# Second layer's values for four heads in one pass: 512 moving columns, three sets of rows in turn

## The chip, the cores and the metric

The kernel runs as one program on one core of a Trainium2 chip. The metric is the device time of one execution in microseconds (us), the median of several runs. A profile of one further execution gives the instructions of each engine: TensorE (PE, with its weight loads listed as PEld), VectorE (DVE), ScalarE (ACT), GpSimd (POOL) and the queue of SyncE (SPq), which issues most of the transfers.

## The reference, cut to what matters

Two decoder layers on 512 tokens of width 2048. The first is gated linear attention and is not touched. The second is multi-head latent attention with 16 heads; the part that matters is how queries, keys and values of the heads come out of two latent rows of width 512, and the attention over them:

```
q = (rms_norm(c_q, g_qa) @ w_qb).reshape(B, S, MLA_HEADS, MLA_NOPE + MLA_ROPE)
kv = (rms_norm(c_kv, g_kva) @ w_kvb).reshape(B, S, MLA_HEADS, MLA_NOPE + MLA_V)
k_nope, v = kv[..., :MLA_NOPE], kv[..., MLA_NOPE:]
...
s = jnp.einsum('bqhd,bkhd->bhqk', qb, k).astype(jnp.float32) * scale
p = jax.nn.softmax(s, axis=-1).astype(v.dtype)
return jnp.einsum('bhqk,bkhv->bqhv', p, v)
```

In w_kvb each head has 256 columns: first 128 for its key, then 128 for its value. The output of the 16 heads is multiplied by a gate and goes through an output projection.

## The kernel before

All large products are made in float32 accuracy by splitting each operand into a high part (type fp32r) and a low rest, and adding three products: high by high, low by high, high by low. The helper mm3 (L123 to L127) issues these three matmuls, so each product of a 128 by 128 stationary tile with its moving rows costs three matmuls and three weight loads, on lines 125, 126 and 127. A matrix from DRAM is loaded in chunks of 1024 numbers a row by the SP queue (tag "raw", three buffers), cast to its high part by ACT (L110, or L827 in the second layer's pairs) and turned into its low part by DVE (L111, L828); the split chunks have four buffers for each part. A finished accumulator of 128 by 512 is split in the same way by split_from: ACT on L174, DVE on L175.

The method mla runs the second layer. After the latent rows cq and ckv and the gates, the heads go in eight pairs. project(p) makes queries, keys and values of pair p, attend(p) does the attention of its two heads; the order in the program is project(0), attend(0), project(1), attend(1) and so on, and after attend(7) the output projection (accumulators yo_acc). The order in which each engine gets its instructions isn't this one: a planner with a simulated timeline (TileContext with schedule_with_timeline_sim) lays it down when the kernel is built, and it moves later work forward into gaps where data and buffers allow. Each engine then runs its own list in that fixed order.

One project(p) holds:

- three accumulators q_acc of 512 columns, 12 matmuls each (four latent tiles by three). The first of them to be made carries the rotary part; its evacuation (L861 to L870) goes through two buffers of the tag "tmp", of which there are six, shared with the softmax rows "pr" of the attention.
- two accumulators k_acc, one for each head, 12 matmuls each with the latent rows (512 columns) as the moving side.
- the values, two accumulators v_acc. Here the latent rows are the stationary side (128 tokens at a time) and the weights move: for each of four blocks of 128 tokens and each of four latent tiles, three matmuls with 256 moving columns, 128 for each of the pair's two heads. Two token blocks share one accumulator. These are 48 matmuls in a pair and 384 in the layer.

The weights for keys and values of a pair come as two chunks by pair_chunk (L816 to L829), each with four transfers of 128 KB. Each chunk holds the keys' and the values' columns of both heads for two latent tiles.

The accumulators named come from a pool of three (tag "mm"). Results lie in rows of act_hi and act_lo, 16 rows of 128 by 512 each, which held the layer's input before. With b = 0 for even pairs and 6 for odd ones, rows b and b+1 hold the queries, b+2 and b+3 the keys, b+4 and b+5 the values (so 4 and 5, or 10 and 11); 12 and 13 hold the rotary queries of even and odd pairs, 14 the rotary key, and 15 is free after the gates. A pair's rows are written again two pairs later, when their last readers are through: for queries and keys the scores (sc, five matmuls for each of four blocks of tokens in a head), for values the product of probabilities and values (o_t).

attend(p) does for each head: scores, mask, maximum, exponential and scaling (L908 to L918, on DVE and ACT), transposition of the probabilities by PE (pt, L927, single matmuls of 128 columns), their split, and the 12 matmuls o_t.

At the end of mla each head's gated output is split into y_hi and y_lo (L729, L730). Head 0's pair of tiles takes the buffers b24 and b25, heads 1 to 8 those of the latent rows, head 9 those of cosine and sine, heads 10 to 15 rows 0 to 5 of act_hi and act_lo. The output projection begins with head 0.

Of the kernel before, what the change touches and what calls it, by code (L numbers as in the profile page):

```python
# [14 lines left out]
F32 = DT.float32  # L15
FR = DT.float32r
# [7 lines left out]
P = 128  # L24
S = 512
D = 2048
ST = S // P
# [12 lines left out]
NOPE = 128  # L40
ROPE = 64
RANK = 512
RK = RANK // P
# [27 lines left out]
class Trunk:  # L71
# [744 lines left out]
    def pair_chunk(self, w, c0, hd, cut, k0):  # L816
# [11 lines left out]
        nc.vector.tensor_tensor(lo, raw, hi.bitcast(F32), ALU.subtract)  # L828
        return hi, lo  # L829

    def project(self, p):

        nc, v, a = self.nc, self.nc.vector, self.a
        par = p % 2
        if p == 0:
            self.key_rope_split()
            self.pairs = {}
        ah, al = self.act_hi, self.act_lo
        b = par * 6
        qn = [(ah[:, b + i, :], al[:, b + i, :]) for i in range(2)]  # L840
        kn = [(ah[:, b + 2 + i, :], al[:, b + 2 + i, :]) for i in range(2)]
        vv = [(ah[:, b + 4 + s // 2, (s % 2) * 256:(s % 2) * 256 + 256],
               al[:, b + 4 + s // 2, (s % 2) * 256:(s % 2) * 256 + 256]) for s in range(ST)]
        qr = [ah[:, 12 + par, :], al[:, 12 + par, :]]
        self.pairs[p] = (qn, kn, vv, qr)

        ps = [self.acc(f"q_acc{i}") for i in range(3)]
        ch = [self.pair_chunk(a["l1_mla_w_qb"], p * 2 * (NOPE + ROPE), NOPE + ROPE, NOPE, k0)
              for k0 in (0, 2)]
        for i in (2, 0, 1):  # L850
            c = slice(i * P, (i + 1) * P)
            for k in range(RK):
                wh, wl = ch[k // 2]
                self.mm3(ps[i], wh[:, k % 2, c], wl[:, k % 2, c], self.cq[0][k], self.cq[1][k],
                         k == 0, k == RK - 1)
            if i < 2:
                self.split_from(ps[i], *qn[i])
            else:
                sw = self.tmp([P, S], F32, "qr_sw")
                for g in range(4):  # L860
                    nc.scalar.copy(sw[32 * g:32 * g + 32], ps[i][32 * (g ^ 1):32 * (g ^ 1) + 32, :])  # L861
                t = self.tmp([P, S], F32, "qr_t")
                v.tensor_tensor(t, ps[i], self.cos, ALU.mult)
                v.tensor_tensor(sw, sw, self.sin, ALU.mult)
                v.tensor_tensor(t, t, sw, ALU.add)
                A, B = slice(0, ROPE), slice(ROPE, P)
                nc.scalar.copy(qr[0][A], t[A])
                v.tensor_tensor(qr[0][B], t[A], qr[0][A].bitcast(F32), ALU.subtract)
                nc.scalar.copy(qr[1][B], t[B])
                v.tensor_tensor(qr[1][A], t[B], qr[1][B].bitcast(F32), ALU.subtract)  # L870

        ch = [self.pair_chunk(a["l1_mla_w_kvb"], p * 4 * NOPE, 2 * NOPE, NOPE, k0) for k0 in (0, 2)]
        for i in range(2):
            pk = self.acc(f"k_acc{i}")
            c = slice(i * P, (i + 1) * P)
            for k in range(RK):
                wh, wl = ch[k // 2]
                self.mm3(pk, wh[:, k % 2, c], wl[:, k % 2, c], self.ckv[0][k], self.ckv[1][k],
                         k == 0, k == RK - 1)
            self.split_from(pk, *kn[i])  # L880
        for s2 in range(2):
            pv = self.acc(f"v_acc{s2}")
            for i in range(2):
                r = slice((s2 * 2 + i) * P, (s2 * 2 + i + 1) * P)
                for k in range(RK):
                    wh, wl = ch[k // 2]
                    self.mm3(pv[:, i * 256:(i + 1) * 256], self.ckv[0][k][:, r], self.ckv[1][k][:, r],
                             wh[:, k % 2, 256:512], wl[:, k % 2, 256:512], k == 0, k == RK - 1)
            self.split_from(pv, ah[:, b + 4 + s2, :], al[:, b + 4 + s2, :])

    def attend(self, p):
        nc, v, te = self.nc, self.nc.vector, self.nc.tensor
# [90 lines left out]
```

## Time and profile before

| what | value |
|---|---|
| median of three runs | 1489.88 us (1489.2 to 1490.59) |
| the profiled execution | 1490.05 us |
| its span, from the first to the last instruction | 1488.3 us |
| granted TensorE clock | 0.999 |
| instructions | 18065 |
| matmuls v_acc<-pw in the second layer | 384 with 256 columns, from 1065.4 to 1288.5 us |

So the profiled execution lies within the runs, 0.17 us above their median, and 1.75 us of it lie outside the span. In the rows of the profile the first number of a listing is the start of an instruction in microseconds from the span's start and the second its duration; since matmuls overlap in the array, what one costs is read from the distance to the start of the next, not from its duration.

### The profile page before, as it was taken

How to read it: one execution, taken by the hardware profiler on the slowest of the kernel's cores; microseconds unless marked ns; L12 is line 12 of the kernel's file. 1: busy time of each engine (PE TensorE's matmuls, PEld its weight loads, DVE VectorE, ACT ScalarE, POOL GpSimd, SP SyncE). 2: the span in 40 equal slices, each digit the busy share in tenths (PEclk: the TensorE clock that was granted, in tenths of full speed). 3: DMA queues.
4: the chain of work that ended last, by engine and by line, in shares of the span. 5: the costliest groups of instructions: out<-in, count | busy, mean ns of one | idle time of the engine just before them, and what ended most of it. 6: DMA issues, size and time to landing. Idle time of an engine off the chain costs nothing.

```text
span 1488.3 us, 18065 instructions
## 1 busy us (share of the span) xinstructions
PE 1472.6 (99%) x7050; PEld 1235.8 (83%) x7050; DVE 738.0 (50%) x1229; ACT 625.7 (42%) x1109; POOL 32.5 (2%) x67
## 2 busy tenths in 40 slices
PE   8999999999999999999999999999999999999998
PEld 6788888888888888888888888888888998888886
DVE  7553644354435454443365444333577777763334
ACT  7432631243124323232254344324666676752221
POOL 2000000000000000100011000000000000000000
PEclk9999999999999999999999999999999999999999
DMA  7323233323331333433262333333322112135223
GB/s 258 104 85 101 70 95 90 100 71 88 97 100 57 100 99 113 134 118 124 92 212 76 107 98 89 99 99 93 83 72 56 51 50 80 59 127 180 92 96 114
DMA packets 110918, 149.85 MB, mean 101 GB/s; under 512 B 17632, under 2 KB 58784, under 8 KB 109808
## 3 DMA queue, kind: packets, MB, share of 16 engines
q1 hardware_dynamic: 107280, 136.86, 30.2%
q0 software_dynamic: 3264, 11.73, 2.3%
q8 instruction: 55, 0.90, 0.3%
q14 instruction: 31, 0.25, 0.1%
q10 hardware_dynamic: 288, 0.09, 0.0%
HBM read 140.08 MB, written 8.59 MB: 100 GB/s over the span
## 4 chain that ended last, share of the span: by engine, by line
PE 95%; DMA 2%; DVE 1%; ACT 1%; issue 1%; SPq 0%; DVEq 0%; ACTq 0%
PE acc L127 11%; PE acc L126 11%; PE acc L125 11%; PE yo_acc L125 8%; PE yo_acc L127 8%; PE yo_acc L126 8%; PE v_acc L127 5%; PE v_acc L126 5%; PE v_acc L125 5%; PE o_t L126 1%; PE o_t L127 1%; PE q_acc L126 1%; PE q_acc L127 1%; PE q_acc L125 1%; PE o_t L125 1%; PE pt L927 1%
## 5 line engine op out<-in xcount | busy, mean ns | idle before, releaser
L111 DVE TENSOR_TENSOR w_lo<-w_raw,w_hi 128x1024 fp32r<-128x1024 f32 x159 | 194.4, 1223 | 379.9 <-ACT w_hi L110 379.5
L110 ACT CAST w_hi<-w_raw 128x1024 fp32r<-128x1024 f32 x159 | 167.3, 1053 | 429.1 <-PE acc L127 186.7
L126 PE MATMUL acc<-act_hi,w_lo 128*128 128x512 f32 x768 | 300.2, 391 | 0.0
L125 PE MATMUL acc<-act_hi,w_hi 128*128 128x512 f32 x768 | 299.6, 390 | 0.0
L127 PE MATMUL acc<-act_lo,w_hi 128*128 128x512 f32 x768 | 298.6, 390 | 0.0
L126 PEld LDWEIGHTS acc<-act_hi,w_lo 128*128 128x128 f32 x768 | 144.2, 188 | 30.6 <-issue 0.7
L127 PEld LDWEIGHTS acc<-act_lo,w_hi 128*128 128x128 f32 x768 | 144.2, 188 | 30.4 <-issue 0.7
L125 PEld LDWEIGHTS acc<-act_hi,w_hi 128*128 128x128 f32 x768 | 144.2, 188 | 29.9
L125 PE MATMUL yo_acc<-w_hi,act_hi 128*128 128x512 f32 x352 | 137.5, 391 | 0.0
L126 PE MATMUL yo_acc<-w_hi,act_lo 128*128 128x512 f32 x352 | 137.1, 389 | 0.0
L127 PE MATMUL yo_acc<-w_lo,act_hi 128*128 128x512 f32 x352 | 137.1, 391 | 0.0
L119 DVE SCALAR_TENSOR_TENSOR w_lo<-w_raw,gcol,w_hi 128x512 fp32r<-128x512 f32 x89 | 63.2, 747 | 101.1 <-ACT w_hi L118 101.0
L118 ACT ACTIVATE w_hi<-w_raw,gcol 128x512 fp32r<-128x512 f32 x89 | 59.8, 716 | 112.0 <-PE acc L127 83.8
L125 PE MATMUL v_acc<-w_hi,act_hi 128*128 128x512 f32 x256 | 100.1, 395 | 6.5 <-DVE w_hi L267 6.4
L126 PE MATMUL v_acc<-w_hi,act_lo 128*128 128x512 f32 x256 | 99.5, 393 | 0.0
L127 PE MATMUL v_acc<-w_lo,act_hi 128*128 128x512 f32 x256 | 97.0, 393 | 0.2 <-DVE w_lo L111 0.2
L127 PEld LDWEIGHTS yo_acc<-w_lo,act_hi 128*128 128x128 f32 x352 | 66.1, 188 | 13.9 <-issue 0.2
L126 PEld LDWEIGHTS yo_acc<-w_hi,act_lo 128*128 128x128 f32 x352 | 66.1, 188 | 13.7
L125 PEld LDWEIGHTS yo_acc<-w_hi,act_hi 128*128 128x128 f32 x352 | 66.1, 188 | 13.7 <-issue 0.2
L125 PEld LDWEIGHTS v_acc<-w_hi,act_hi 128*128 128x128 f32 x256 | 48.6, 190 | 17.2 <-issue 6.3
L126 PE MATMUL yo_acc<-w_hi,y_lo 128*128 128x512 f32 x160 | 62.5, 391 | 0.0
L125 PE MATMUL yo_acc<-w_hi,y_hi 128*128 128x512 f32 x160 | 62.4, 391 | 0.0
(301 smaller groups left out, 2458.4 us busy)
## 6 DMA issues: line engine op xcount, KB each, us to landing
w_raw<-in_l_gla_w_in_dram SPq DMA_DIRECT2D x63, 512.0 KB, 3.8
w_raw<-in_l_mla_w_in_dram SPq DMA_DIRECT2D x47, 512.0 KB, 3.6
w_raw<-in_l_gla_w_in_dram SPq DMA_DIRECT2D x66, 256.0 KB, 3.1
w_raw<-in_l_gla_w_out_dram SPq DMA_DIRECT2D x32, 512.0 KB, 3.8
w_raw<-in_l_mla_w_out_dram SPq DMA_DIRECT2D x32, 512.0 KB, 3.6
pw_raw<-in_l_mla_w_kvb_dram SPq DMA_DIRECT2D x64, 128.0 KB, 2.4
xo<-in_x_dram POOLq DMA_DIRECT2D x16, 256.0 KB, 6.0
x1d<-yo SPq DMA_DIRECT2D x4, 1024.0 KB, 5.6
```

The source lines that it names most:

```text
L110: nc.scalar.copy(hi, raw)
L111: nc.vector.tensor_tensor(lo, raw, hi.bitcast(F32), ALU.subtract)
L118: nc.scalar.activation(hi[:, kk, :], raw[:, kk, :], AF.Copy, scale=g)
L119: nc.vector.scalar_tensor_tensor(lo[:, kk, :], raw[:, kk, :], g, hi[:, kk, :].bitcast(F32), ALU.mult, ALU.subtract)
L125: t.matmul(out, lh, rh, start=start, stop=False)
L126: t.matmul(out, ll, rh, start=False, stop=False)
L127: t.matmul(out, lh, rl, start=False, stop=stop)
L927: te.transpose(pt[:, o:o + P], probs[i][:, j * P:(j + 1) * P], self.ident)
```

## The change

Values are now made once for two pairs, in the even project. There all four heads' value columns lie side by side, so one matmul moves 512 columns, and each block of 128 tokens fills an accumulator of its own: four accumulators of 12 matmuls. The odd project makes queries and keys alone. A finished accumulator is split in two halves, one for each pair. The new kv_chunk loads keys or values alone: the keys of a pair as one chunk with two transfers, the values of four heads as two chunks with four transfers each; it calls chunk_split (L100), which does the same cast and subtraction as pair_chunk did.

Values of up to three pairs exist at a time now, and lie in three sets of rows that are taken in turn by the pair's number: set 0 is rows 4 and 5, set 1 rows 10 and 11, set 2 is row 15 of act_hi and of act_lo for the two high parts and buffers b24 and b25 for their low parts. So pairs 2 and 5 use b24 and b25, which later take head 0's split output.

```
+    def kv_chunk(self, c0, n, k0, nk):
+        w = self.a["l1_mla_w_kvb"]
+        raw = self.wp.tile([P, nk, n * NOPE], F32, tag="raw", name="kv_raw", bufs=3)
+        for h in range(n):
+            c = c0 + h * 2 * NOPE
+            self.nc.sync.dma_start(raw[:, :, h * NOPE:(h + 1) * NOPE],
+                                   w[k0 * P:(k0 + nk) * P, c:c + NOPE].rearrange("(k p) n -> p k n", p=P))
+        return self.chunk_split(raw)
+    def value_rows(self, i):
+        ah, al = self.act_hi, self.act_lo
+        if i < 2:
+            return [(ah[:, r, :], al[:, r, :]) for r in ((4, 5), (10, 11))[i]]
+        return [(t[:, 15, :], self.slot(b, [P, S], FR, "v_lo")) for t, b in ((ah, "b24"), (al, "b25"))]
...
-        vv = [(ah[:, b + 4 + s // 2, (s % 2) * 256:(s % 2) * 256 + 256],
-               al[:, b + 4 + s // 2, (s % 2) * 256:(s % 2) * 256 + 256]) for s in range(ST)]
+        if par == 0:
+            self.v_rows = [self.value_rows((p + q) % 3) for q in range(2)]
+        vv = [tuple(t[:, (s % 2) * 256:(s % 2) * 256 + 256] for t in self.v_rows[par][s // 2])
+              for s in range(ST)]
...
-        ch = [self.pair_chunk(a["l1_mla_w_kvb"], p * 4 * NOPE, 2 * NOPE, NOPE, k0) for k0 in (0, 2)]
+        wh, wl = self.kv_chunk(p * 4 * NOPE, 2, 0, RK)
         for i in range(2):
...
-        for s2 in range(2):
-            pv = self.acc(f"v_acc{s2}")
-            for i in range(2):
-                r = slice((s2 * 2 + i) * P, (s2 * 2 + i + 1) * P)
-                for k in range(RK):
-                    wh, wl = ch[k // 2]
-                    self.mm3(pv[:, i * 256:(i + 1) * 256], self.ckv[0][k][:, r], self.ckv[1][k][:, r],
-                             wh[:, k % 2, 256:512], wl[:, k % 2, 256:512], k == 0, k == RK - 1)
-            self.split_from(pv, ah[:, b + 4 + s2, :], al[:, b + 4 + s2, :])
+        if par:
+            return
+        ch = [self.kv_chunk(p * 4 * NOPE + NOPE, 4, k0, 2) for k0 in (0, 2)]
+        for s in range(ST):
+            pv = self.acc(f"v_acc{s}")
+            r = slice(s * P, (s + 1) * P)
+            for k in range(RK):
+                wh, wl = ch[k // 2]
+                self.mm3(pv, self.ckv[0][k][:, r], self.ckv[1][k][:, r], wh[:, k % 2, :], wl[:, k % 2, :],
+                         k == 0, k == RK - 1)
+            o = (s % 2) * 256
+            for q in range(2):
+                vh, vl = self.v_rows[q][s // 2]
+                self.split_from(pv[:, q * 256:(q + 1) * 256], vh[:, o:o + 256], vl[:, o:o + 256])
```

More of the change, by code (lines that the diff above doesn't have):

```diff
@@ L876, in project @@
             for k in range(RK):
-                wh, wl = ch[k // 2]
-                self.mm3(pk, wh[:, k % 2, c], wl[:, k % 2, c], self.ckv[0][k], self.ckv[1][k],
+                self.mm3(pk, wh[:, k, c], wl[:, k, c], self.ckv[0][k], self.ckv[1][k],
                          k == 0, k == RK - 1)
             self.split_from(pk, *kn[i])
-        for s2 in range(2):
-            pv = self.acc(f"v_acc{s2}")
-            for i in range(2):
-                r = slice((s2 * 2 + i) * P, (s2 * 2 + i + 1) * P)
-                for k in range(RK):
-                    wh, wl = ch[k // 2]
-                    self.mm3(pv[:, i * 256:(i + 1) * 256], self.ckv[0][k][:, r], self.ckv[1][k][:, r],
-                             wh[:, k % 2, 256:512], wl[:, k % 2, 256:512], k == 0, k == RK - 1)
-            self.split_from(pv, ah[:, b + 4 + s2, :], al[:, b + 4 + s2, :])
+        if par:
[12 more added lines that the diff above has]
+                self.split_from(pv[:, q * 256:(q + 1) * 256], vh[:, o:o + 256], vl[:, o:o + 256])
     def attend(self, p):
```

## The prediction

> **What bounds the kernel now.** I read the page's busy times first, then PE's waits in the second layer's heads (1050 to 1350 us), then the busy times of that stage by windows.
>
> ```profile
> span 1488.3 us, 18065 instructions
> ...
> PE 1472.6 (99%) x7050; PEld 1235.8 (83%) x7050; DVE 738.0 (50%) x1229; ACT 625.7 (42%) x1109; POOL 32.5 (2%) x67
> ...
> PEclk9999999999999999999999999999999999999999
> ```
>
> ```profile
> PE k_acc L125 <- DVE qr_t L863: 0.3, 1, 0.3
> ```
>
> ```profile
> 1140.00:1160.00 20.00, 20.00 (x124) 17.99 (x123) 14.78 (x44) 13.73 (x35) 0.00 (x0) 1.00 0.18 47
> ...
> sum 300.00, PE 299.71 PEld 264.70 DVE 209.50 ACT 195.79 POOL 1.11; mean PE 19.98 PEld 17.65 DVE 13.97 ACT 13.05 POOL 0.07
> ```
>
> The reader is to see three things. PE is busy for 99% of the span at the full clock. In the 300 us around the heads its waits come to one of 0.3 us. DVE is busy for 209.5 of the 300 us (70%) and ACT for 195.8 (65%), so neither is the bound. In the heads, time is the sum of what each matmul holds the array for, and a change counts as far as it alters that sum or makes PE wait.
>
> The busy share can't tell how long a matmul holds the array, since matmuls overlap. That is read from the distance between starts in PE's listing: a run of value matmuls, one of query matmuls as the stage begins, one in the thick of it.
>
> ```profile
> 1065.37 0.28 PE L125 MATMUL v_acc<-pw_hi,ckv_hi 128*128 128x256 f32 x1
> ...
> 1068.12 0.28 PE L127 MATMUL v_acc<-pw_lo,ckv_hi 128*128 128x256 f32 x1
> ...
> 1055.04 0.39 PE L127 MATMUL q_acc<-cq_lo,pw_hi 128*128 128x512 f32 x1
> ...
> 1058.89 0.39 PE L126 MATMUL q_acc<-cq_hi,pw_lo 128*128 128x512 f32 x1
> ...
> 1105.62 0.39 PE L125 MATMUL q_acc<-cq_hi,pw_hi 128*128 128x512 f32 x1
> ...
> 1108.16 0.39 PE L127 MATMUL q_acc<-cq_lo,pw_hi 128*128 128x512 f32 x1
> ```
>
> The first two rows are the ends of 24 matmuls in a row, 23 distances: 2.75 / 23 = 0.1196 us for 256 columns. The next two have 17 distances, 3.85 / 17 = 0.2265 us for 512 columns; the last two 11 distances, 2.54 / 11 = 0.2309 us. So 512 columns cost less than twice 256, by 0.0127 or by 0.0083 us. If a matmul costs a part for its columns and a fixed part, the fixed part is 8 to 13 ns.
>
> **The value matmuls.**
>
> ```profile
> L125 PE MATMUL v_acc<-pw_hi,ckv_hi 128*128 128x256 f32 x128 | 36.4, 284 | 0.0
> ```
>
> Three lines of 128 make 384 matmuls of 256 columns: 384 x 0.1196 = 45.9 us of PE's time. Afterwards there are 4 even projects x 4 accumulators x 12 = 192 matmuls of 512 columns: 43.5 us at 0.2265, 44.3 us at 0.2309. As PE has no slack, the difference falls on the path: a saving of 2.4 or 1.6 us. I take the middle, 2.0 us, since both kinds of stretch occur in the stage. The number of columns moved is the same, 98,304; what goes is 192 fixed parts.
>
> The Trainium skill speaks against the size of this gain: its page "TensorE: Matmul & The Clock Gate", section "Back-to-back issue gap", gives the warm distance as the columns divided by 2.4 GHz plus about 2.5 ns. By that the gain would be 192 x 2.5 ns, an estimate of 0.5 us from the page. The rows above show 8 to 13 ns instead, and I go by them.
>
> **What the matmuls stand next to.** PE's lists will be laid out anew by the planner, and where a group of transpositions breaks into other work there is a price:
>
> ```profile
> 1082.42 0.30 PE L927 MATMUL pt<-cf,pr 128*128 128x128 f32 x1
> ...
> 1302.58 0.62 PE L927 MATMUL pt<-cf,pr 128*128 128x128 f32 x4
> 1302.96 0.48 PE L126 MATMUL yo_acc<-w_hi,y_lo 128*128 128x512 f32 x1
> 1303.28 0.39 PE L127 MATMUL yo_acc<-w_lo,y_hi 128*128 128x512 f32 x1
> ...
> 1340.12 0.49 PE L927 MATMUL pt<-cf,pr 128*128 128x128 f32 x3
> ```
>
> The matmul after a group holds the array for 0.32 us where 0.23 is usual: 0.09 us for each break. Between the first and the last of these rows I count 62 breaks in the listing. There can't be fewer than 48 (three groups in each of 16 heads) and I allow as many more, 76: 1.3 us either way. I take none.
>
> **Evacuation.** ACT and DVE split 32 halves of 256 columns instead of 16 accumulators of 512.
>
> ```profile
> L174 ACT CAST act_hi<-v_acc 128x512 fp32r<-128x512 f32 x16 | 9.3, 583 | 2.4 <-PE v_acc L127 2.3
> L174 ACT CAST pt_h<-pt 128x384 fp32r<-128x384 f32 x32 | 15.3, 480 | 5.3 <-PE pt L927 4.8
> L175 DVE TENSOR_TENSOR act_lo<-v_acc,act_hi 128x512 fp32r<-128x512 f32 x16 | 11.0, 686 | 5.2 <-ACT act_hi L174 5.2
> L175 DVE TENSOR_TENSOR pt_l<-pt,pt_h 128x384 fp32r<-128x384 f32 x32 | 17.2, 548 | 2.7 <-ACT pt_h L174 2.7
> ```
>
> No row has 256 columns in this form. Drawn on from 512 to 384, it comes to 377 ns on ACT and 410 ns on DVE, which is an estimate. Then ACT has 12.1 instead of 9.3 us and DVE 13.1 instead of 11.0. That is 2 to 3 us over 260, on engines with 30% to spare: nothing on the path. An accumulator is free after about 1.2 us (two casts and the last subtraction, 0.38 + 0.38 + 0.41) where it was 1.27; PE needs 12 x 0.23 = 2.7 us to fill one, and the layer fills 14 of them in two pairs as before (7 + 7, now 9 + 5). No loss.
>
> **Weights.**
>
> ```profile
> L827 ACT CAST pw_hi<-pw_raw 128x1024 fp32r<-128x1024 f32 x16 | 16.0, 1045 | 6.9 <-DMA pw_raw<-in_l_mla_w_qb_dram 4.6 <-PE v_acc L126 2.3
> L828 DVE TENSOR_TENSOR pw_lo<-pw_raw,pw_hi 128x1024 fp32r<-128x1024 f32 x16 | 19.0, 1217 | 5.0 <-ACT pw_hi L827 5.0
> ...
> w_raw<-in_l_gla_w_in_dram SPq DMA_DIRECT2D x66, 256.0 KB, 3.1
> ...
> pw_raw<-in_l_mla_w_kvb_dram SPq DMA_DIRECT2D x64, 128.0 KB, 2.4
> ```
>
> Four chunks of 1024 numbers a row for two pairs before, four after (one of keys for each pair, two of values): the same casts and subtractions. SP issues 48 transfers instead of 64, 16 of 256 KB and 32 of 128 KB; by these rows the larger land in 3.1 instead of 2.4 us. PE waits for no weights here, so this costs nothing. An even project needs five chunks where four buffers exist (two of queries, one of keys, two of values), so the last value chunk waits until a query chunk is used up: its 1.05 + 1.22 us of splitting lies behind 24 matmuls of keys, 5.5 us. Without that cover it would cost 2.3 us in each of four projects.
>
> **Rows.** Pair p's values take the set of pair p-3, where they took the rows of pair p-2. An even project therefore waits for o_t of pair p-2 at the latest (the set that pair p+1 gets), which is the wait it had. Behind the waiting splits on ACT and DVE stand the softmax steps of the attention then running. Head 0's output can't be split early any more (it was, at 1106 us): b24 and b25 are pair 5's values until its o_t is over.
>
> ```profile
> 1274.88 0.27 PE L127 MATMUL o_t<-pt_l,act_hi 128*128 128x128 f32 x1
> ...
> 1289.17 0.39 PE L125 MATMUL yo_acc<-w_hi,y_hi 128*128 128x512 f32 x1
> ```
>
> That is the last of pair 5 and the first that needs head 0: 14.3 us between them for a cast and a subtraction. Nothing on the path, unless pair 5 slips by more than that.
>
> **The sum.** 1490.05 - 2.0 = 1488.05 us for the profiled execution. That stood 0.17 above the median of the runs, so against the median: 1489.88 - 2.0 = 1487.9 us. With the bounds of both terms the forecast's own range is 1489.88 - 2.4 - 1.3 = 1486.2 to 1489.88 - 1.6 + 1.3 = 1489.6. A measurement of this kernel can tell about 0.2%, 3.0 us, from no change, and 2.0 lies below it.
>
> **Rivals.** *PE starves in odd projects (slower).* The work that fills PE's gaps while attention waits for softmax becomes uneven.
>
> ```profile
> 1130.89 0.28 PE L127 MATMUL v_acc<-pw_lo,ckv_hi 128*128 128x256 f32 x1
> ...
> 1162.73 0.28 PE L127 MATMUL v_acc<-pw_lo,ckv_hi 128*128 128x256 f32 x1
> ...
> L174 ACT CAST pt_h<-pt 128x512 fp32r<-128x512 f32 x16 | 9.4, 586 | 27.7 <-PE pt L927 27.7
> ```
>
> These are the last value matmuls of pairs 2 and 3: a pair takes 31.8 us. Without values (48 x 0.1196 = 5.7 us) an odd one has 26.1 us of PE work; an even one has 26.1 + 48 x 0.229 = 37.1. If the attention can't run faster than it does now, PE idles up to 5.7 us in each of four odd periods. Halfway, 2.9 us each, gives 11.4 - 2.0 = 9.4 us more: 1499.3. It decides from 1.25 us of idling in each odd period, where the change is 3.0 us slower. For it: queries of the next pair but one can't be evacuated before the scores of the running pair have read their rows. Against it: ACT waited 27.7 us for transpositions by PE, so the attention is paced by PE and not the other way, and DVE, busy for 209.5 / 300 of 31.8 = 22.2 us a pair, would in an odd period have 22.2 - 1.4 - 1.2 = 19.6 us of 26.1 (less two splits of values and one chunk of weights). Chance 0.18.
>
> *The planner's new order has fewer breaks.* At 48 breaks and the quiet pitch: 2.4 + 1.3 = 3.7 us saved, 1486.2. For it: longer runs of one kind; against it: nothing in the program joins transpositions. Chance 0.14.
>
> *The fixed part is small.* If value matmuls of 512 columns ran at 0.2367 us (as 0.1196 x 2 less 2.5 ns), 0.5 us would be saved: 1489.4. For it: 512 columns already differ between 0.2265 and 0.2309 by what runs beside them. Against it: no run here is that slow. It is the outcome of the page's rule above. Chance 0.06.
>
> **How the numbers follow.** The forecast has 0.62, of which 0.08 lie beyond 3.0 us. With the planner's luck, faster is 0.08 + 0.14 = 0.22. Starving gives slower, 0.16 of its 0.18; the other 0.02 and the small fixed part are within 0.2%: 0.54 + 0.02 + 0.06 = 0.62. The range, 1485.5 to 1491.5, holds the forecast, the two rivals beside it and the lightest starving (up to 0.9 us of idling in each odd period: 1487.9 + 3.6 = 1491.5), and leaves out most of that rival and a little luck beyond the bounds.
>
> **What would show it.** Right: 192 matmuls v_acc of 512 columns, 0.2265 to 0.2309 us apart; PE's waits in the heads under 1 us; all heads over some 2 us earlier; 62 breaks give or take 14. Wrong: PE waiting for q_acc, sc or o_t in odd projects, a first yo_acc that waits for y_hi, or a pitch over 0.235.

## The result: slower, by half a per cent

The changed kernel takes 1497.06 us (median of six runs, 1496.63 to 1499.72) against 1489.81 for the kernel before: 1.0052 times as long, with a 95% interval of 1.0042 to 1.0062. That is 7.25 us more, outside the predicted range and on the other side from the forecast. The profiled execution, with 1499.72 us, is the longest of the six, 2.7 us above their median. Medians here and below leave out two executions far longer than the others of their kernel (3558 us in e8, 1633 us in e14).

The page of the changed kernel, and PE's waits in the heads (1050 to 1350 us):

```profile
span 1497.9 us, 17673 instructions
...
PE 1475.7 (99%) x6858; PEld 1227.4 (82%) x6858; DVE 737.6 (49%) x1245; ACT 627.9 (42%) x1125; POOL 32.6 (2%) x67
```

```profile
PE sc L125 <- ACT pr L939: 2.9, 2, 1.6
PE yo_acc L126 <- DVE y_lo L730: 0.6, 1, 0.6
PE k_acc L125 <- DVE act_lo L175: 0.5, 2, 0.3
PE o_t L125 <- ACT pt_h L174: 0.5, 2, 0.3
PE q_acc L125 <- DVE act_lo L175: 0.5, 1, 0.5
PE k_acc L125 <- DVE qr_t L882: 0.3, 1, 0.3
...
```

The 192 matmuls less are there (6858 for 7050), and the busy share still reads 99%: in a span longer by 9.6 us it tells nothing. The waits tell: one of 0.3 us has become nine groups. The largest is new in kind, scores (sc) that wait for the softmax (pr) of earlier scores. Where they lie is seen from the windows, where the number behind the comma is PE's busy time; first the kernel before, then the changed one:

```profile
1050.00:1250.00 200.00, 199.71 (x1178) 177.50 (x1177) 143.35 (x329) 135.98 (x286) 0.00 (x0) 1.00 0.24 65
1250.00:1350.00 100.00, 100.00 (x559) 87.37 (x558) 66.49 (x143) 59.34 (x120) 4.28 (x8) 1.00 0.27 94
```

```profile
1050.00:1250.00 200.00, 198.75 (x1017) 169.00 (x1016) 140.54 (x327) 133.29 (x285) 0.00 (x0) 1.00 0.25 68
1250.00:1350.00 100.00, 95.25 (x488) 79.84 (x486) 65.80 (x158) 63.59 (x138) 3.03 (x6) 0.98 0.24 82
```

PE idles 1.25 us in the first 200 us and 4.75 in the last 100. Busy time counts overlapping matmuls, so I also added up, from PE's listing, by how much each distance between two starts exceeds the usual one for that size (0.2275 us for 512 columns, 0.1196 for 256, 0.1735 for 384, 0.06 or 0.112 for 128, 0.09 more behind transpositions). I call this the lost time; the usual distances are rounded, so a few us stand there without any wait. In us:

```
stage             before   changed   difference
1050 to 1280         3.5       6.5       +3.0
1280 to 1330         0.9       9.2       +8.3
1330 to 1360         0.1       0.4       +0.3
```

The 11.6 us of difference less 2.0 us of value time give the 9.6 us between the two spans of the profiled executions. So the loss lies mainly in the last two attentions, when the last project is through.

### The profile page after: what moved, and what is told of

Same layout as the page of the kernel before. It is cut to its first block, busy times and chain, and to the rows that moved or that the text cites. A ratio compares the mean times of both kernels' runs of the same rounds, so it can differ in the third digit from the quotient of the medians.

```text
span 1497.9 us, 17673 instructions
## 1 busy us (share of the span) xinstructions
PE 1475.7 (99%) x6858; PEld 1227.4 (82%) x6858; DVE 737.6 (49%) x1245; ACT 627.9 (42%) x1125; POOL 32.6 (2%) x67
## 4 chain that ended last, share of the span: by engine, by line
PE 92%; DVE 3%; ACT 2%; DMA 1%; issue 1%; SPq 0%; DVEq 0%; ACTq 0%
PE acc L127 11%; PE acc L125 11%; PE acc L126 11%; PE yo_acc L126 8%; PE yo_acc L125 8%; PE yo_acc L127 8%; PE v_acc L127 4%; PE v_acc L125 4%; PE v_acc L126 4%; PE o_t L126 1%; PE o_t L127 1%; PE o_t L125 1%; PE q_acc L125 1%; PE q_acc L126 1%; PE q_acc L127 1%; PE ckv_acc L125 1%
## 5 line engine op out<-in xcount | busy, mean ns | idle before, releaser
L126 PE MATMUL acc<-act_hi,w_lo 128*128 128x512 f32 x768 | 300.4, 391 | 0.0
L125 PE MATMUL acc<-act_hi,w_hi 128*128 128x512 f32 x768 | 299.8, 390 | 0.0
L126 PEld LDWEIGHTS acc<-act_hi,w_lo 128*128 128x128 f32 x768 | 144.2, 188 | 30.6 <-issue 0.7
L125 PEld LDWEIGHTS acc<-act_hi,w_hi 128*128 128x128 f32 x768 | 144.2, 188 | 29.7
L125 PE MATMUL yo_acc<-w_hi,act_hi 128*128 128x512 f32 x352 | 137.5, 391 | 0.0
L126 PE MATMUL yo_acc<-w_hi,act_lo 128*128 128x512 f32 x352 | 137.2, 390 | 0.0
L125 PE MATMUL v_acc<-w_hi,act_hi 128*128 128x512 f32 x256 | 100.2, 396 | 7.1 <-DVE w_hi L267 6.6
L126 PE MATMUL v_acc<-w_hi,act_lo 128*128 128x512 f32 x256 | 99.6, 393 | 0.0
L125 PEld LDWEIGHTS yo_acc<-w_hi,act_hi 128*128 128x128 f32 x352 | 66.1, 188 | 13.8 <-issue 0.2
L126 PEld LDWEIGHTS yo_acc<-w_hi,act_lo 128*128 128x128 f32 x352 | 66.1, 188 | 13.5
L126 PE MATMUL yo_acc<-w_hi,y_lo 128*128 128x512 f32 x160 | 62.8, 392 | 0.6 <-DVE y_lo L730 0.6
L125 PEld LDWEIGHTS v_acc<-w_hi,act_hi 128*128 128x128 f32 x256 | 48.6, 190 | 17.8 <-issue 6.6
L125 PE MATMUL yo_acc<-w_hi,y_hi 128*128 128x512 f32 x160 | 62.7, 392 | 0.0
```

The costliest lines, as they stand in the source:

```text
L125: t.matmul(out, lh, rh, start=start, stop=False)
L126: t.matmul(out, ll, rh, start=False, stop=False)
```

## Experiments

Each run's ratio is to the kernel before on the same chip, whose median was 1489.7 to 1489.8 in all of them. In some kernels a line of the helpers stands one lower (L126 for L125).

**First theory: the end lacks pair 7's values.** Project 7 no longer has values to fill PE's gaps. The rival was that every odd project starves. The joined pairs were set by a table of how many pairs' values each project makes; a project with one pair does it as the kernel before, in the rows of set p % 3.

```
+GROUP = {0: 2, 2: 2, 4: 2, 6: 1, 7: 1}                        # e1
+GROUP = {0: 1, 1: 1, 2: 1, 3: 1, 4: 1, 5: 1, 6: 2}            # e2
```

> Pairs 0 to 5 get their values as in the changed kernel (144 matmuls of 512 columns in projects 0, 2 and 4), pairs 6 and 7 each in their own project with 256 columns, as before. Theory A (the loss lies at the end: with the values of pair 7 gone from project 7, the last two attentions lack work that fills PE's gaps): the 8 us lost between 1280 and 1330 us come back, three quarters of the 2.0 us of value time stay saved, and the 1 us that odd projects 1, 3 and 5 each lost stays lost: 1490 us, within 1489 to 1491.5. Theory B (every odd project starves alike): three of four losses stay, 1495 us or more. Theory C (the new planning as such costs, wherever): no more than a quarter of 7.3 us comes back.

Measured: 1497.79 us, 1.0053 (1.0040 to 1.0065). Nothing came back, as the rivals B and C both had it.

> Pairs 0 to 5 each get their values in their own project with 256 columns, as before (but in the three sets of rows in turn); only pairs 6 and 7 get them together, in project 6, with 512 columns. Theory A (the loss lies at the end): the end loses as in the changed kernel, some 8 us, and 0.5 us are saved: 1496 to 1498 us. Theory B (each odd project starves alike): a quarter of the loss, 1491 to 1492. If the three sets of rows themselves cost, this and the run with pairs 6 and 7 apart would both be slower than their sum allows.

Measured: 1490.70 us, 1.0006 (0.9997 to 1.0014). Joining the last two pairs, where the theory put the loss, costs next to nothing. The theory falls, twice. This kernel also takes the three sets of rows in turn, so these cost no more than that by themselves. But the place of the loss stays: with the last pairs apart, PE's lost time is again 7.6 us from 1280 to 1330, and PE's longest waits in the heads (1050 to 1350 us), the first two of them in that stretch, read

```profile
PE yo_acc L126 <- DVE qr_t L886: 1.8, 1, 1.8
PE sc L126 <- ACT pr L961: 1.2, 2, 0.9
PE k_acc L126 <- DVE act_lo L176: 0.8, 1, 0.8
```

**The price of the fixed part.** Each value matmul of the changed kernel as two of 256 columns:

```
-            for k in range(RK):
+            for i in range(2):
+                c = slice(i * 256, (i + 1) * 256)
+                for k in range(RK):
...
+                    self.mm3(pv[:, c], self.ckv[0][k][:, r], self.ckv[1][k][:, r],
+                             wh[:, k % 2, c], wl[:, k % 2, c], k == 0, k == RK - 1)
```

> The changed kernel with each value matmul of 512 columns done as two of 256 (four heads in one accumulator, all else as it is). This prices the fixed part of a matmul: 192 more matmuls at 8 to 13 ns are 1.6 to 2.4 us more than the changed kernel, if the planner keeps the order, so 1498.7 to 1499.5. With the fixed part of 2.5 ns it would be 0.5 us more. If the extra work fell into gaps where PE starves, nothing would be added.

Measured: 1494.29 us, 1.0032 (1.0021 to 1.0044): 2.8 us less than the changed kernel with 192 matmuls more. The planner's order is another one here. The lost time is 3.9 us up to 1280, like that of the kernel before, and 5.3 instead of 9.2 from 1280 to 1330. As a price for the fixed part the run is useless; it shows that how the order falls out is worth more than the term I had worked out. It is also a warning for what follows: every edit brings a new order, so a single step of 1 to 3 us can come from that alone.

**Too little work at the end.** The output projection's first block has four accumulators, one for each block of tokens. The fourth is the buffer "mm_x", which one score in three also uses (sc_x). Until the last sc_x is through, only three token blocks can be computed, and the four weight chunks in the buffers are held for the fourth: 4 chunks x 2 tiles x 3 blocks x 3 = 72 matmuls, 16.4 us. In PE's listing exactly 72 yo_acc stand before the last sc_x in the kernel before, in the changed one and in e1, e2 and e3. The last of the 72 and the last sc_x, before and then changed:

```profile
1310.26 0.39 PE L127 MATMUL yo_acc<-w_lo,y_hi 128*128 128x512 f32 x1
...
1312.68 0.28 PE L907 MATMUL sc_x<-act_lo 128*128 128x256 f32 x1
```

```profile
1314.12 0.47 PE L127 MATMUL yo_acc<-w_lo,y_hi 128*128 128x512 f32 x1
...
1323.83 0.28 PE L931 MATMUL sc_x<-act_lo 128*128 128x256 f32 x1
```

In the kernel before 2.4 us lie between the two, in the changed one 9.7 us, in which PE has the attention alone.

```
-                if (4 * hh + i) % 3 == 2:
+                if (4 * hh + i) % 3 == 2 and p < 7:
```

> The changed kernel, but the scores of the last pair use only their two own accumulators and not the third one (sc_x), which is the output projection's fourth accumulator. Theory A1 (the end starves since only three of four accumulators of the output projection are to be had before the last scores are through, so just 4 chunks x 18 = 72 of its matmuls can fill gaps, and the weight buffers stay held): the fourth accumulator comes free after pair 6, the fill goes on, and 3 to 6 us of the 7.3 come back: 1491 to 1494. Theory A2 (it is the softmax chain of the last pair that is too long, whatever fills): no gain, or a loss of 1 to 2 us as the last scores have one accumulator less.

Measured: 1494.07 us, 1.0031 (1.0020 to 1.0042): 3.0 us back, as theory A1 had it. From 1290 on nothing is lost any more; what stays, 3.8 us, lies from 1280 to 1290.

There the changed kernel's listing shows the next cause: the last o_t of pair 5, the split of head 0's low part (from DVE's listing), and the matmul that waits for it.

```profile
1289.35 0.28 PE L127 MATMUL o_t<-pt_l,act_lo 128*128 128x128 f32 x1
...
1291.26 0.50 PE L126 MATMUL yo_acc<-w_hi,y_lo 128*128 128x512 f32 x1 [0.59 <-DVE y_lo L730]
```

```profile
1290.53 0.68 DVE L730 TENSOR_TENSOR y_lo<-msg,y_hi 128x512 fp32r<-128x512 f32 x1
```

Pair 5's values sit in b24 and b25, and head 0, with which the output projection begins, gets b25 for its low part only after pair 5's last products. DVE isn't idle in the 1.2 us after them: a split, a mask and a maximum stand ahead of this one in its list, so part of the wait is for its place there. Two kernels tell this apart, the second with both edits:

```
-            if h < 1:
+            if h == 8:
                 th, tl = self.slot("b24", [P, S], FR, "y_hi"), self.slot("b25", [P, S], FR, "y_lo")
-            elif h < 9:
-                th = self.slot(f"b{2 * h - 2}", [P, S], FR, "y_hi")
-                tl = self.slot(f"b{2 * h - 1}", [P, S], FR, "y_lo")
+            elif h < 8:
+                th = self.slot(f"b{2 * h}", [P, S], FR, "y_hi")
+                tl = self.slot(f"b{2 * h + 1}", [P, S], FR, "y_lo")
```

> The changed kernel, but heads 0 to 7 put their split outputs in the buffers of the latent rows and head 8 takes b24 and b25, so that the output projection's first matmuls no longer wait for the last reader of pair 5's values. Theory F (part of the end's loss, from 1280 to 1291 us, is that wait: y_lo of head 0 was split at 1290.5, 1.2 us after the last o_t of pair 5): 2 to 4 us come back, 1493 to 1495. Without it, nothing: 1497.

Measured: 1495.66 us, 1.0037 (1.0024 to 1.0050). The 1.4 us gained are less than expected, and the interval overlaps that of the changed kernel, so this run alone doesn't show a gain. A likely reason is that the 72 matmuls are just used up earlier: in the trace the loss from 1280 to 1300 is gone, and from 1300 to 1330 it has grown to 7.0.

> The changed kernel with both: head 0's output not in b24 and b25, and the last pair's scores on two accumulators, so that the output projection gets its fourth one before them. If the end's loss is lack of work beside the last attentions, the two gains add: 3.0 us (measured for the second alone) plus 2 to 4, 1490 to 1492.5, and PE's waits between 1280 and 1330 us fall under 2 us. If they are the same gain, 1494.

Measured: 1490.44 us, 1.0004 (0.9996 to 1.0013). Both together bring back 6.6 of the 7.25 us, more than their sum of 4.4. With the scores' edit in place (1494.07) that of head 0 is worth 3.6 us, clear of the noise. PE's busy time in the same windows as above:

```profile
1050.00:1250.00 200.00, 198.75 (x1019) 168.84 (x1018) 140.27 (x327) 133.20 (x288) 0.00 (x0) 1.00 0.25 67
1250.00:1350.00 100.00, 99.80 (x516) 84.97 (x515) 68.04 (x156) 64.17 (x134) 1.11 (x2) 1.00 0.26 84
```

PE's 198.75 us in the first row are the changed kernel's to the hundredth; the second has 99.80 for 95.25. Is that a gain of the two edits as such?

> The kernel before with the two edits (head 0's output not in b24 and b25, the last pair's scores on two accumulators). The kernel before has work beside its last attentions: its PE loses only 0.9 us more than usual in the last 50 us of the heads. Theory G (the two edits only give back what the change lost there): 1489.7, within 0.7. If they are a gain of their own, 1487 or less, and the changed kernel with both edits would have to be held against that.

Measured: 1489.93 us, 1.0001 (0.9992 to 1.0010). In the kernel before they do nothing. They only give back what the change lost.

**Why the end is short of work.** In the kernel before, 15.6 us of the attention's matmuls are left when the last project is through (scores, transpositions and o_t after the last k_acc or v_acc, counted with the usual distances). In the changed one it is 22.5, and the work beside them is no more than before. The count goes with the loss but doesn't set its size: it gives 18 us for e1, e2 and e3 as well, which lost 7.6, 1.8 and 5.3 us at the end. The attention is late from the start: the last o_t of pair 0, before and after,

```profile
1116.86 0.27 PE L127 MATMUL o_t<-pt_l,act_hi 128*128 128x128 f32 x1
```

```profile
1125.44 0.28 PE L127 MATMUL o_t<-pt_l,act_hi 128*128 128x128 f32 x1
```

comes 8.6 us later, and that of pair 5 14.5 us later (1289.35 for 1274.88). Two kernels ask whether one early delay is enough, and whether joining other pairs avoids it:

```
+GROUP = {0: 2, 2: 1, 3: 1, 4: 1, 5: 1, 6: 1, 7: 1}            # e11
+GROUP = {0: 1, 1: 2, 3: 2, 5: 2, 7: 1}                        # e5
```

> Only pairs 0 and 1 get their values together, in project 0; all others alone with 256 columns, in the three sets of rows. Theory D (the 5.7 us of values put ahead of the first attention make it late, and the delay is carried to the end): the first o_t ends some 6 us later than before and the last pairs are still late; 1491 to 1494. If attention catches up within two pairs: 0.5 us saved, 1489.3 plus or minus 0.7.

Measured: 1495.25 us, 1.0039 (1.0027 to 1.0051). Joining pairs 0 and 1 alone, 5.7 us of work (as the kernel before does it) drawn forward once, costs 5.5 us. The last o_t of pairs 0 and 5 in this kernel:

```profile
1122.00 0.27 PE L128 MATMUL o_t<-pt_l,act_hi 128*128 128x128 f32 x1
...
1282.39 0.27 PE L128 MATMUL o_t<-pt_l,act_lo 128*128 128x128 f32 x1
```

They are 5.1 and 7.5 us late, though all pairs after the first two are as before: the delay isn't made up in 160 us. Attention work left at the last project: 18.1 us.

> Four heads at once for pairs 1 and 2, 3 and 4, 5 and 6 (in projects 1, 3 and 5), pairs 0 and 7 alone with 256 columns as before. 144 matmuls of 512 columns save 1.5 us. Theory D (the attention falls behind the projects because values are made ahead of it, from the first project on, and at the end the work left for it has too little beside it): here nothing extra stands before the first attention and project 7 keeps its own values, so the attention left when the projects are through is near the 15.6 us of before, and most of the loss goes: 1488.5 to 1492. Theory E (any uneven planning makes the attention fall behind, wherever the values are joined): 1495 to 1498, as with the last pairs apart.

Measured: 1496.44 us, 1.0045 (1.0033 to 1.0057). The time is the one of theory E: joining these pairs brings nearly the same loss. The first attention is only 2.5 us late (last o_t at 1119.4), but pair 5's is 11.2 us late; 18.0 us are left. So a delay of the first attention is enough for a loss, as e11 shows, but isn't needed. "Any uneven planning" goes too far, though: e2 is one, and lost next to nothing, with pair 5's last o_t 3.8 us late.

> Only pairs 0 and 1 joined, with both edits. Theory D (the delay of the first attention is carried to the end and costs there): the 3.3 us lost between 1300 and 1330 us come back, 1495.25 - 3.3 = 1492, and 1490 or less if the 2 us that k_acc of the last project lost go too. If the delay cost elsewhere, 1494 or more.

Measured: 1492.07 us, 1.0018 (1.0009 to 1.0026): 3.2 us back, as theory D said. What stays is one place, 3.9 us lost from 1270 to 1280, where k_acc of project 7 waits 1.8 us for a split by DVE. Another 1.7 us of it are the clock, of which the last section has more: from 1275 to 1280 us the granted clock was 0.69, the 5 us before 0.97.

> Only pairs 6 and 7 joined, with both edits. Alone it stood at 1490.7 with 1.8 us lost between 1300 and 1320. With the loss gone and 48 matmuls of 512 in the place of 96 of 256 (0.5 us): 1488.9 to 1489.4, the fastest so far.

Measured: 1489.50 us, 0.9997 (0.9988 to 1.0006): with the end mended, the joined last pairs are level with the kernel before, on the side that the 0.5 us of saving has, and not distinguishable from it.

**The rest: 1490.4 where 2.0 us are saved.**

> The changed kernel with both edits and each value matmul of 512 columns done as two of 256. With PE no longer short of work at the end, the 192 extra fixed parts of 10.5 ns (the distance in the changed kernel's trace is 0.2285 us, against two times 0.1195) should now show: 1490.4 + 2.0 = 1492.4, less up to 3 us if the planner's order here has none of the small waits in odd projects, as the kernel with halves alone had none: 1489.4 to 1492.4.

Measured: 1490.42 us, 1.0003 (0.9994 to 1.0012), the same as with 512 columns (1490.44). PE is full here, as the windows show:

```profile
1050.00:1250.00 200.00, 199.70 (x1183) 177.75 (x1182) 141.74 (x333) 135.13 (x290) 0.00 (x0) 1.00 0.25 67
1250.00:1350.00 100.00, 100.00 (x549) 86.56 (x548) 65.95 (x151) 61.41 (x128) 1.11 (x2) 1.00 0.25 85
```

The kernel with 512 columns has the shorter matmuls and loses 2.8 us more up to 1280 (6.5 for 3.7); the two cancel. Those losses gather round waits of q_acc, o_t and k_acc near 1167, 1204, 1236 and 1278 us, 0.5 to 0.8 us at each. The first three lie in stretches between two runs of values, the fourth behind the last run, where PE has only queries and keys to put beside the attention; those at 1167 and 1236 are in even projects (4 and 6), ahead of their values. With halves, in an order of its own, none of them occurs. A guess at their cause was that the rotary accumulator holds one of three:

```
-        for i in (2, 0, 1):
+        for i in (0, 1, 2):
```

> The changed kernel with both edits, and the rotary query accumulator made last of the three instead of first. Theory H (in odd projects, with no values to make, queries and keys cycle through two accumulators since the rotary one is held until softmax buffers come free, and PE waits for their splits): the rotary one is held for 5.5 us less, some of the 3 us lost in odd projects come back: 1487.8 to 1489.5. If the waits have another cause, 1490.4 or, by another order, up to 1492.

Measured: 1490.53 us, 1.0005 (0.9996 to 1.0014). The guess falls: the waits for act_lo are gone and two others have come.

```profile
PE o_t L125 <- ACT pt_h L174: 2.4, 2, 1.5
```

The first, 0.9 us at 1237.6, is again between two runs of values; the longer, at 1307.5, lies in the last attentions. So the two edits don't keep the end free of waits in every order: in e9, e14, e15 and e16 next to nothing is lost from 1280 to 1330 us, here some 1.8 us.

> The kernel before with the same three edits (both, and the rotary accumulator last). The kernel before loses next to nothing in its projects (PE's waits there are 0.3 us), so theory H gives no gain: 1489.8 plus or minus 0.7. If this gains as much as the changed kernel does, the order as such is the gain and the change still brings nothing.

Measured: 1489.22 us, 0.9996 (0.9987 to 1.0005). No difference from the kernel before, as expected; by its median it is the fastest of all, 0.5 us under the kernel before, which can't be told from none. No version found beats the kernel before by more than can be told. What sets the waits between the runs of values is open: one order has them, another has others, and the one with halves has none.

## Why the prediction was wrong

**The value matmuls: right.** A run of 20 in project 6:

```profile
1255.39 0.39 PE L126 MATMUL v_acc<-w_hi,ckv_lo 128*128 128x512 f32 x1
...
1259.70 0.39 PE L127 MATMUL v_acc<-w_lo,ckv_hi 128*128 128x512 f32 x1
```

4.31 / 19 = 0.2268 us; over all 151 distances within longer runs 0.2285, against 2 x 0.1195 before. 192 x 10.5 ns are the 2.0 us of the sum. The 2.5 ns that the Trainium skill's page "TensorE: Matmul & The Clock Gate", section "Back-to-back issue gap", gives for the isolated gap between matmuls do not hold for this stream with a weight load before each.

**Breaks, evacuation, weights: right.** 61 breaks by transpositions (62 before). The halves took 372 ns on ACT and 411 to 425 on DVE (estimates: 377 and 410):

```profile
L174 ACT CAST act_hi<-v_acc x28: 361/372/383, 1069.2 to 1265.9; 128x256 fp32r<-128x256 f32 x28
L175 DVE TENSOR_TENSOR act_lo<-v_acc,act_hi x24: 411/420/425, 1069.8 to 1266.3; 128x256 fp32r<-128x256 f32 x24
```

No wait for a value chunk shows.

**Rows: wrong.** I gave head 0's wait in b24 and b25 a cover of 14.3 us "unless pair 5 slips by more than that". Pair 5 slipped by 14.5, and the first yo_acc, at 1285.17, stands 4 us earlier. With the end's other cause mended, taking head 0 out of these buffers was worth 3.6 us (e9 against e4). I had named the condition and not asked what would move pair 5, though the change itself puts 5.7 us of values ahead of the first attention.

**The sum: this is the step that failed.** It took PE's total as the time, since PE had no slack. That holds while there is other work to put between attention's steps. After project 7 there are 72 matmuls of the output projection, and the kernel before used them up 2.4 us before its last sc_x; with the later attention of the changed kernel it is 9.7 us. PE stays nearly full for 200 us (1.25 us of idling), at the cost of this end: the 8.3 us from 1280 to 1330 in the profiled execution are four times the saving. That this lack of work is the cause is shown by e4 and e9 against e6: giving the end its work back returns 6.6 of the 7.25 us here and nothing in the kernel before. Why the attention falls behind is shown in part: the values ahead of the first attention suffice (e11), but e5 loses nearly as much without them, and why the attention falls behind there stays open.

**The rival was right in kind and wrong in place.** I let PE starve where an odd project has no values, and priced each of these at up to 5.7 us; waits are there, in even projects too, but they lost up to 0.8 us each. Its counter-argument (ACT waited for PE, so PE paces the attention) was true of the average and said nothing of the end. That its halfway price, 1499.3 us, stands near the 1497.06 measured is luck. And I gave 0.18 to all of it.

## What to carry to other kernels

When an engine is full only because later work is drawn forward into its gaps, ask what is left to draw from at the end of the stage, and whether the change moves work out of that reserve; a delay early in such a stage may not be seen before its end. Work made ahead of its need can be paid by those whose turn it takes, even if every engine stays busy. A buffer lent to a new user needs the date of its last reader in the new order, not in the old trace.

## What the runs showed of the hardware

The starving had a second price, the clock. In these windows of the changed kernel the third number from the end is the granted clock:

```profile
1285.00:1290.00 5.00, 3.64 (x21) 2.81 (x20) 5.00 (x15) 2.89 (x10) 0.00 (x0) 1.00 0.10 22
...
1315.00:1320.00 5.00, 3.26 (x16) 2.37 (x15) 4.28 (x15) 3.05 (x9) 0.00 (x0) 0.89 0.01 3
1320.00:1325.00 5.00, 5.00 (x31) 4.82 (x30) 3.14 (x12) 3.50 (x10) 0.00 (x0) 0.77 0.00 0
```

```profile
1319.92 0.63 PE L126 MATMUL o_t<-pt_h,act_lo 128*128 128x512 f32 x1
1320.35 0.63 PE L127 MATMUL o_t<-pt_l,act_hi 128*128 128x512 f32 x1
```

After a stretch in which PE was busy for 3.26 of 5 us the clock fell, and two matmuls of 512 columns stand 0.43 us apart instead of 0.23. By the two windows (0.11 and 0.23 of 5 us) that cost 1.7 us of the 8.3. With the windows laid where the granted clock changes, it reads

```profile
1315.52:1318.93 3.41, 1.67 (x9) 1.13 (x8) 3.41 (x13) 1.52 (x5) 0.00 (x0) 1.00 0.02 5
1318.93:1322.35 3.42, 3.42 (x12) 2.95 (x11) 1.35 (x7) 3.10 (x9) 0.00 (x0) 0.50 0.00 0
```

That is half the clock for 3.41 us. The traces of the heads hold five such falls (here and in e1, e5, e8 and e15), each 3.41 us long and each starting a whole number of these steps after the clock's first rise. In the step ahead of a fall PE was busy for 1.5 to 1.7 us; no step with 1.8 us or more was followed by one. The price isn't in every execution: of the six, the two longest (1498.69 and 1499.72 us) have a mean granted clock of 0.997, while two near the median (1496.83 and 1497.04) have 0.999, as the kernel before. So the 7.25 us between the medians stand largely without it.

The Trainium skill's page "TensorE: Matmul & The Clock Gate", section "What's actually happening", describes a gate that watches how busy PE was in windows of about 3.4 us and gives half the clock after an idle one. This trace agrees on the length and on the half. It differs in the condition: PE was busy for 1.67 us of the window ahead of the fall.
